# The first k-tiles of a two-layer decoder trunk in a written order, and one pair with seven products in place of two in the second group

## The chip, the cores and the metric

One program runs on one core of a Trainium2 chip. The time is the device time of one execution in microseconds (us), taken as the median of several runs. TensorE (PE) multiplies; its weight loads are shown as PEld. VectorE (DVE) and ScalarE (ACT) prepare its operands, GpSimd (POOL) raises to powers, and SyncE (SP) issues the DMAs.

## The reference, cut to what matters

A trunk of two layers on 256 tokens of 2048 values: retention, a SwiGLU feed-forward part, latent attention, and a second feed-forward part, each between two RMS norms. The change touches the first products of the retention alone:

```python
h = rms_norm(x, norm_mix_pre[0])               # x: 256 tokens x 2048
proj = h @ w_in                                # 2048 x (2048 q, 2048 k, 4096 v, 4096 g)
q, k, v, g = split(proj)
q = rope(q, positions)
k = rope(k, positions) * dk ** -0.5
scores = einsum('bhqd,bhkd->bhqk', q, k) * decay_in
```

## The kernel before

**Precision.** Every float32 matrix is split in two parts of a shorter format, hi (a cast, by ScalarE) and lo (the difference, by VectorE; `split`, L207 to L216). A product of two matrices is then three: hi by hi, hi by lo, lo by hi. A k-tile is 128 of the 2048 rows; its weight tile has 128 x 1024 values (512 KB), loaded in one DMA (`tile_load`, L543; `weights`, L218). There are two token tiles (t = 0 and 1) of 128 tokens and two halves of 512 columns (c = 0 and 1), so a k-tile takes 2 x 2 x 3 = 12 matmuls of 512 columns into four of six PSUM banks.

**The input.** x is turned by TensorE transposes in pieces of 2, 2, 4, 4 and 4 k-tiles for each token tile (`PIECES`, L577; `norm_piece`, L598). A piece is transposed into PSUM, multiplied by the norm's gains on VectorE (L608) into a tile of the "mv" slots, split into `hT`, and the squares for the norm's scale are summed one step later on ScalarE (L127). The scale itself is applied to the products afterwards.

**Groups.** The query and key part has four groups of 1024 columns (`qk_group`, L799). The first goes through `group` (L273): 16 k-tiles, all in the plain way, 192 matmuls; a `lead` of 3 lets the second token tile follow some k-tiles behind, and with `halves` = 1 the first weight tile is loaded and split in two halves of 512 columns. The other three go through `first_sevens` (L425): the first pairs of k-tiles (`QK_SEVENS` = 2 of them) are multiplied as 2 x 2 block matrices with seven products in place of eight (three matmuls each, so a pair takes 21 and not 24), the other k-tiles in the plain way. The seven need sums of blocks: of the weights for each group on VectorE (L458 to L473), of x once (`watched`, L581; `left_sums`, L244; up to three pairs are made, as the value and gate groups use three), as soon as both token tiles of a pair are there. Their results are put together in the banks by VectorE sums (L485 to L495) before the plain k-tiles are added.

**Between groups.** After each group its four banks are turned by the rotary tables on VectorE (`rotated`, L811: two multiplications a bank, L822 and L823, and four sums a token tile's two banks, L827 and L828), transposed on TensorE (L846) and multiplied to scores (L856). The tables come from `rotary_tables` (L150) after the first group: some fifteen small VectorE operations and two on ScalarE.

**Order.** The program's text gives each instruction a rank, and a planner with a cost for each instruction gives every engine's order: of what is ready by its costs, the first in the text goes first, so an operation of a later line can go ahead of one that would still wait. `later(k, fn)` (L133) puts work `k` steps on; a step passes with each weight tile that is loaded (`step`, L137). All DMAs are issued by SP in the order of the text: the identity, x of t = 0 (512 columns), the gains, two halves of weight tile 0, x of t = 1, weight tile 1, and so on. At the start 7 matmuls on zeros keep TensorE at work (`use`, L97), and 3 more come between the first transposes. Slots: 4 raw weight tiles, 5 hi and 5 lo ("whi", "wlo"), 6 "mv"; in the query and key part 3 spare tiles besides, of which a group uses one for a raw tile and two for the hi and lo of its last k-tile (`share`, L202).

## Time and profile before

| | |
|---|---|
| median of 3 runs | 2403.68 us (2402.67 to 2405.07) |
| profiled execution | 2402.24 us |
| its span | 2400.5 us |
| TensorE busy | 2383.1 us (99%) |
| VectorE busy | 2171.0 us (90%) |
| ScalarE busy | 1489.9 us (62%) |
| HBM over the span | 192 GB/s |

The span runs from the first to the last instruction; the execution's time has 1.74 us more around it. Busy time counts work and not waits; matmuls overlap, so that a matmul's own duration (about 0.39 us) is longer than the distance to the next. In the rows, `out<-in` names the tiles that an instruction writes and reads; `rqk` is the query and key part, `htp` the transposed x, `hx` that times the gains, `rx` the sums of x, `rope` the turned banks, `rtp` and `rsc` the transposes and products of the scores.

### The profile page before, as it was taken

To read this page: it belongs to the slowest core of one execution; us is meant where nothing else is said; L and a number is where in the kernel's file an instruction comes from. 1 tells how busy PE (TensorE), PEld (TensorE's weight loads), DVE (VectorE), ACT (ScalarE), POOL (GpSimd) and SP (SyncE) were. 2 spreads that over 40 slices of the span, in tenths; PEclk is the share of its full clock that TensorE was granted. 3 is DMA by queue.
4 is the path that set the end of the run, shared out by engine and by line. 5 is a ranking of instruction groups with operands and counts; after the bars stand their busy time and mean duration, and the time that the engine had idled before them with its cause. 6 is when DMAs were issued, how large, how long until landed. Compare 5 with 4: busy or idle time off the path is not lost.

```text
span 2400.5 us, 30798 instructions
## 1 busy us (share of the span) xinstructions
PE 2383.1 (99%) x10849; PEld 1969.1 (82%) x10849; DVE 2171.0 (90%) x3098; ACT 1489.9 (62%) x2104; POOL 28.6 (1%) x38
## 2 busy tenths in 40 slices
PE   9999999999999999999999999999999999999998
PEld 7888888888888888888888888887888888888887
DVE  8878989888899999999989987889999999998998
ACT  6545665665666666666666666656666665666664
POOL 0000000000001000000000000000000000000000
PEclk9999999999999999999999999999999999999999
DMA  8465465445656665656456565445666565655654
GB/s 284 166 206 192 167 209 189 165 168 190 217 187 220 210 211 188 215 180 222 153 194 215 200 197 161 128 141 168 236 200 219 177 220 184 211 166 184 220 199 168
DMA packets 129611, 463.76 MB, mean 193 GB/s; under 512 B 14640, under 2 KB 15024, under 8 KB 129456
## 3 DMA queue, kind: packets, MB, share of 16 engines
q1 hardware_dynamic: 129456, 461.80, 57.6%
q8 instruction: 85, 1.39, 0.2%
q14 instruction: 70, 0.57, 0.1%
HBM read 459.64 MB, written 2.10 MB: 192 GB/s over the span
## 4 chain that ended last, share of the span: by engine, by line
PE 92%; DVE 5%; DMA 1%; ACT 1%; issue 1%; SPq 0%; POOL 0%; DVEq 0%; POOLq 0%; ACTq 0%
PE gu_b L419 35%; PE dn_b L419 15%; PE rvg_b L419 14%; PE rto_b L419 6%; PE rqk_b L419 5%; PE dn_m L419 3%; PE q L419 3%; PE mlo_b L419 2%; PE mc_b L419 1%; PE rto_m L419 1%; PE ftp L981 1%; PE ry L909 1%; DVE xs L671 0%; PE asc L1233 0%; PE asc L1230 0%
## 5 line engine op out<-in xcount | busy, mean ns | idle before, releaser
L419 PE MATMUL gu_b<-gu_w_hi,hT 128*128 128x512 f32 x1296 | 353.5, 390 | 0.1
L419 PEld LDWEIGHTS gu_b<-gu_w_hi,hT 128*128 128x128 f32 x1296 | 242.1, 188 | 50.8 <-DVE hT L211 0.9
L210 ACT CAST dn_w_hi<-dn_w_raw 128x1024 fp32r<-128x1024 f32 (+1 forms) x176 | 169.1, 978 | 78.4 <-DMA dn_w_raw<-w_down 32.8
L419 PE MATMUL gu_b<-gu_w_lo,hT 128*128 128x512 f32 x648 | 200.2, 390 | 0.2 <-DVE gu_w_lo L211 0.2
L211 DVE TENSOR_TENSOR dn_w_lo<-dn_w_raw,dn_w_hi 128x1024 fp32r<-128x1024 f32 (+1 forms) x176 | 193.2, 1128 | 7.1 <-ACT dn_w_hi L210 6.7
L419 PE MATMUL dn_b<-dn_w_lo,dn_ah 128*128 128x512 f32 x494 | 156.7, 389 | 0.0
L419 PE MATMUL dn_b<-dn_w_hi,dn_ah 128*128 128x512 f32 x494 | 156.6, 389 | 0.0
L419 PE MATMUL rvg_b<-rvg_w_hi,hT 128*128 128x512 f32 x576 | 156.5, 390 | 0.0
L419 PE MATMUL dn_b<-dn_w_hi,dn_al 128*128 128x512 f32 x494 | 156.4, 389 | 0.0
L211 DVE TENSOR_TENSOR gu_w_lo<-gu_w_raw,gu_w_hi 128x1024 fp32r<-128x1024 f32 x122 | 143.3, 1217 | 5.3 <-ACT gu_w_hi L210 5.1
L419 PEld LDWEIGHTS gu_b<-gu_w_lo,hT 128*128 128x128 f32 x648 | 121.2, 188 | 26.6 <-DVE gu_w_lo L211 1.6
L210 ACT CAST gu_w_hi<-gu_w_raw 128x1024 fp32r<-128x1024 f32 x122 | 122.5, 1049 | 28.3 <-PE gu_b L419 11.0
L419 PEld LDWEIGHTS rvg_b<-rvg_w_hi,hT 128*128 128x128 f32 x576 | 107.8, 188 | 22.3
L210 ACT CAST gu_ahi<-gu_ta 128x1024 fp32r<-128x1024 f32 x80 | 84.4, 1055 | 46.7 <-PE gu_b L419 36.2
L211 DVE TENSOR_TENSOR gu_clo<-gu_s,gu_chi 128x1024 fp32r<-128x1024 f32 x80 | 97.4, 1219 | 14.7 <-ACT gu_chi L210 13.4
L419 PEld LDWEIGHTS dn_b<-dn_w_lo,dn_ah 128*128 128x128 f32 x494 | 92.7, 188 | 19.6 <-DVE dn_w_lo L211 0.4
L419 PEld LDWEIGHTS dn_b<-dn_w_hi,dn_al 128*128 128x128 f32 x494 | 92.7, 188 | 19.3
L419 PEld LDWEIGHTS dn_b<-dn_w_hi,dn_ah 128*128 128x128 f32 x494 | 92.7, 188 | 19.2
L419 PE MATMUL rqk_b<-rqk_w_hi,hT 128*128 128x512 f32 x384 | 106.0, 392 | 2.5 <-ACT rqk_w_hi L210 1.9
L211 DVE TENSOR_TENSOR gu_alo<-gu_ta,gu_ahi 128x1024 fp32r<-128x1024 f32 x80 | 97.7, 1221 | 6.4 <-ACT gu_ahi L210 6.4
L210 ACT CAST gu_bhi<-gu_s 128x512 fp32r<-128x512 f32 x80 | 49.7, 622 | 78.1 <-PE gu_b L419 63.2
L210 ACT CAST gu_chi<-gu_s 128x1024 fp32r<-128x1024 f32 x80 | 83.8, 1051 | 13.5 <-PE gu_b L419 13.5
(534 smaller groups left out, 6251.6 us busy)
## 6 DMA issues: line engine op xcount, KB each, us to landing
dn_w_raw<-w_down SPq DMA_DIRECT2D x176, 512.0 KB, 4.5
gu_s<-w_gu SPq DMA_DIRECT2D x160, 512.0 KB, 4.6
gu_w_raw<-w_gu SPq DMA_DIRECT2D x152, 512.0 KB, 3.7
rvg_w_raw<-ret_vg SPq DMA_DIRECT2D x67, 512.0 KB, 4.4
rto_w_raw<-ret_out SPq DMA_DIRECT2D x64, 512.0 KB, 4.3
rvg_s<-ret_vg SPq DMA_DIRECT2D x48, 512.0 KB, 4.2
rqk_w_raw<-ret_qk SPq DMA_DIRECT2D x47, 512.0 KB, 4.6
gu_w_xraw<-w_gu SPq DMA_DIRECT2D x40, 512.0 KB, 5.3
```

The costliest lines, as they stand in the source:

```text
L210: nc.scalar.copy(out=hi, in_=src)
L211: nc.vector.tensor_sub(out=lo, in0=src, in1=hi.bitcast(F32))
L419: nc.tensor.matmul(out, e[2](), e[3](), start=bank not in begun, stop=ends[bank, added.get(bank, 0)] == n, skip_group_check=bank in added,)
L909: nc.tensor.matmul(y, left, right, start=n == 0, stop=n == len(terms) - 1)
L981: nc.tensor.transpose(tp[:, b * P : (b + 1) * P], a[:, b * P : (b + 1) * P], ident)
```

## The change

The first five k-tiles of the first group, and the start, get a written order. `begin` opens a manual order for TensorE, VectorE and ScalarE. x of both token tiles is loaded in 256 columns first, between the two halves of weight tile 0, and the other 256 columns after weight tile 1; all go through SP as before. Of k-tile 0 both token tiles are multiplied by the first column half before the second half's turn. The transposes of the second pieces stand before the last three matmuls of k-tile 0, those of the third pieces behind k-tile 1. From k-tile 5 on the planner orders again; `lead` is 1. The pieces of the first eight k-tiles are kept in two spare tiles (not in "mv" slots), so this group's last k-tile has no spare room for its hi and lo. The squares of these pieces come 6 steps later, of the others 2. The sums of x come later: of the first pair 6 steps after its pieces, of the second and third 22 and 24, which is in the second group. So this group has one pair with seven products (`QK_SEVENS` = 0, 1, 2, 2), its other 14 k-tiles are plain. The rotary tables are made at k-tile 8 of the first group, the constants loaded at k-tile 6. The first group's score transposes and products come three steps later than those of the others. 6 and 2 matmuls on zeros stand in place of 7 and 3; the load of the activation table stands behind the first DMAs in the text.

```diff
 MLO_SEVENS = (3, 5), (1, 3)
-QK_SEVENS, VG_SEVENS = 2, 3
+QK_SEVENS, VG_SEVENS = (0, 1, 2, 2), 3
...
-    use(7)
+    use(6)
...
     nc.sync.dma_start(out=cst[:, C_ID : C_ID + P], in_=consts[:, C_ID : C_ID + P])
+    nc.sync.dma_start(out=xs[:, 0, 0:256], in_=xv[:, 0, 0:256])
+    nc.sync.dma_start(out=gcol, in_=gains)
+    nc.scalar.preload_act_table_set("silu_and_others")
     ident = cst[:, C_ID : C_ID + P]
...
-        def run(t, kt, cs):
-            for i, j in ((0, 0), (0, 1), (1, 0)):
+        def run(t, kt, cs, order=((0, 0), (0, 1), (1, 0))):
+            for i, j in order:
                 for c in cs:
...
         held = [[], []]
-        for kt in range(kts):
-            plan.append(("do", lambda kt=kt: load_one(kt)))
+        done, loaded = (0, 0) if begin is None else begin(plan, run, load_one, w)
+        for kt in range(done, kts):
+            if kt >= loaded:
+                plan.append(("do", lambda kt=kt: load_one(kt)))
             if kt // 2 in sevens:
...
-    def watched(pairs):
+    def watched(pairs, wait=None):
...
                     if (1 - t, p) in held:
-                        f, hi, lo = tiles[0](len(made))
-                        left_sums(*held[0, p], *held[1, p], f, hi, lo)
-                        made[p] = hi, lo
+                        if wait is None:
+                            make(p)
+                        else:
+                            later(wait(p), lambda p=p: make(p))
+        def make(p):
+            f, hi, lo = tiles[0](len(made))
+            left_sums(*held[0, p], *held[1, p], f, hi, lo)
+            made[p] = hi, lo
         watch[0] = seen
         return made, tiles
-    def norm_piece(t, i, ssq, col):
+    def norm_piece(t, i, ssq, col, room=None, wait=1):
+        norm_parts(t, i, ssq, col, room, wait)()
+    def norm_parts(t, i, ssq, col, room=None, wait=1):
         k0, n = PIECES[i]
...
         ks = slice(k0 % 4, k0 % 4 + n)
-        part = wp.tile([P, 512], F32, tag="mv", bufs=MV, name=f"hx{t}{i}")
-        part = part[:, 0 : n * P].rearrange("p (j q) -> p j q", j=n)
+        if room is None:
+            part = wp.tile([P, 512], F32, tag="mv", bufs=MV, name=f"hx{t}{i}")[:, 0 : n * P]
+        else:
+            part = room(t, k0, n)
+        part = part.rearrange("p (j q) -> p j q", j=n)
         nc.vector.tensor_tensor(
             out=part, in0=tp[:, 0 : n * P].rearrange("p (j q) -> p j q", j=n),
             in1=gcol[:, col + k0 : col + k0 + n][:, :, None].to_broadcast([P, n, P]), op=ALU.mult,
         )
-        split(hx(k0)[:, ks, 0, t, :], hx(k0)[:, ks, 1, t, :], part)
-        if watch[0] is not None:
-            watch[0](t, k0, n, part)
-        later(1, lambda: squares(xs[:, t, k0 * P : (k0 + n) * P], ssq[:, i : i + 1]))
+        def rest():
+            split(hx(k0)[:, ks, 0, t, :], hx(k0)[:, ks, 1, t, :], part)
+            if watch[0] is not None:
+                watch[0](t, k0, n, part)
+            def part_squares():
+                ins = squares(xs[:, t, k0 * P : (k0 + n) * P], ssq[:, i : i + 1])
+                if wait > 1:
+                    tc.keep_in_program_order(ins)
+            later(wait, part_squares)
+        return rest
...
+        def load_half(t, i):
+            sl = slice(i * 256, (i + 1) * 256)
+            nc.sync.dma_start(out=xs[:, t, sl], in_=xv[:, t, sl])
         def load_constants():
...
             lo = wp.tile([P, 4, P], F32R, tag="al", bufs=3, name="rxl")
             return f, hi, lo
-        ins, where = watched(max(QK_SEVENS, VG_SEVENS))
+        ins, where = watched(VG_SEVENS, lambda p: 6 + 2 * p if p < 1 else 20 + 2 * p)
         where[0] = tiles
-        load_x(0, 0)
-        later(0, lambda: norm_piece(0, 0, first[0], G_MIX))
-        later(0, lambda: norm_piece(0, 1, first[0], G_MIX))
-        later(0, lambda: use(3))
-        nc.sync.dma_start(out=gcol, in_=gains)
-        for k, c, t in ((1, 0, 1), (2, 1, 0), (3, 1, 1), (5, 2, 0), (6, 2, 1), (8, 3, 0), (9, 3, 1)):
+        pieces, spare_q = {}, [None]
+        def first_room(t, k0, n):
+            if k0 // 4 not in pieces:
+                pieces[k0 // 4] = spare_q[0](F32, f"hx{k0}")
+            a = t * 512 + k0 % 4 * P
+            return pieces[k0 // 4][:, a : a + n * P]
+        def first_parts(t, i):
+            return norm_parts(
+                t, i, first[t], G_MIX, first_room if i < 3 else None, 6 if i < 3 else 2
+            )
+        def begin(plan, run, load, w):
+            ordered = ExitStack()
+            parts = {}
+            def do(fn, *args):
+                plan.append(("do", lambda: fn(*args)))
+            def loads():
+                step()
+                ordered.enter_context(
+                    tc.manual_schedule(engines={nc.tensor.engine, nc.vector.engine, nc.scalar.engine})
+                )
+                raw = wp.tile([P, 1024], F32, tag="raw", bufs=RAW, name="rqk0_w0_raw")
+                hi = wp.tile([P, 1024], F32R, tag="whi", bufs=WB, name="rqk0_w0_hi")
+                lo = wp.tile([P, 1024], F32R, tag="wlo", bufs=WB, name="rqk0_w0_lo")
+                w[0] = hi, lo, raw
+                nc.sync.dma_start(out=raw[:, 0:512], in_=ret_qk[0, 0, :, 0:512])
+                load_half(1, 0)
+                nc.sync.dma_start(out=raw[:, 512:1024], in_=ret_qk[0, 0, :, 512:1024])
+            def half(c):
+                split(*(x[:, c * 512 : (c + 1) * 512] for x in w[0]))
+            def transposed(t, i):
+                parts[t, i] = first_parts(t, i)
+            def made(t, i):
+                parts[t, i]()
+            do(loads)
+            do(transposed, 0, 0)
+            do(use, 2)
+            do(made, 0, 0)
+            do(transposed, 1, 0)
+            do(half, 0)
+            do(made, 1, 0)
+            do(half, 1)
+            run(0, 0, (0,), ((0, 0), (1, 0)))
+            run(1, 0, (0,), ((0, 0),))
+            run(0, 0, (0,), ((0, 1),))
+            run(1, 0, (0,), ((0, 1), (1, 0)))
+            run(0, 0, (1,), ((0, 0), (1, 0), (0, 1)))
+            do(load, 1)
+            for t in range(NT):
+                do(load_half, t, 1)
+            for t in range(NT):
+                do(transposed, t, 1)
+            run(1, 0, (1,), ((0, 0), (1, 0), (0, 1)))
+            for t in range(NT):
+                do(made, t, 1)
+            do(load, 2)
+            do(load, 3)
+            for kt in range(1, 5):
+                for t in range(NT):
+                    run(t, kt, (0, 1))
+                if kt == 1:
+                    for t in range(NT):
+                        do(transposed, t, 2)
+                if kt < 3:
+                    do(load, kt + 3)
+                if kt == 1:
+                    for t in range(NT):
+                        do(made, t, 2)
+            do(ordered.close)
+            return 5, 6
+        for k, c, t in ((2, 1, 0), (3, 1, 1), (5, 2, 0), (6, 2, 1), (8, 3, 0), (9, 3, 1)):
             later(k, lambda c=c, t=t: load_x(c, t))
-        later(10, load_constants)
-        for k, t, i in (
-            (2, 1, 0), (2, 1, 1), (3, 0, 2), (3, 1, 2),
-            (7, 0, 3), (7, 1, 3), (10, 0, 4), (10, 1, 4),
-        ):
-            later(k, lambda t=t, i=i: norm_piece(t, i, first[t], G_MIX))
+        later(6, load_constants)
+        later(8, rotary_tables)
+        for k, t, i in ((6, 0, 3), (6, 1, 3), (10, 0, 4), (10, 1, 4)):
+            later(k, lambda t=t, i=i: first_parts(t, i)())
         def qk_group(gq, spare):
             name = f"rqk{gq}"
             if gq:
-                return first_sevens(h_lhs, DT, ret_qk, gq, name, QK_SEVENS, lambda p: ins[p], spare)
-            return group(h_lhs, DT, tile_load(ret_qk, gq, name, 1, spare), name, lead=3)
+                return first_sevens(h_lhs, DT, ret_qk, gq, name, QK_SEVENS[gq], lambda p: ins[p], spare)
+            return group(h_lhs, DT, tile_load(ret_qk, gq, name, 0, spare), name, lead=1, begin=begin)
         def vg_group(h, spare):
             return first_sevens(h_lhs, DT, ret_vg, h, f"rvg{h}", VG_SEVENS, lambda p: ins[p], spare)
...
+                wait = 0 if gq else 3
                 for t in range(NT):
                     for c in range(2):
-                        later(2 + t, lambda t=t, c=c: transposes(t, c))
+                        later(wait + 2 + t, lambda t=t, c=c: transposes(t, c))
                 for h2 in range(2):
-                    later(5, lambda h2=h2: products(h2))
+                    later(wait + 5, lambda h2=h2: products(h2))
             with tc.tile_pool(name="rt_q", bufs=1) as rp:
                 rope_c = rp.tile([P, NT, NF_R], F32, name="rope_c")
                 rope_s = rp.tile([P, NT, NF_R], F32, name="rope_s")
-                spare = share(3, lambda kind, name: rp.tile([P, 1024], kind, tag="spare", bufs=3, name=name))
+                spare_q[0] = lambda kind, name: rp.tile([P, 1024], kind, tag="spare", bufs=3, name=name)
+                spare = share(3, spare_q[0])
                 for gq in range(4):
-                    banks = qk_group(gq, spare)
+                    banks = qk_group(gq, spare if gq else (1, 0, spare_q[0]))
                     if gq == 0:
                         rx = [rms(first[t], D, "rx", f"first_r{t}") for t in range(NT)]
-                        rotary_tables()
                         for t in range(NT):
```

## Rows read from the trace of the kernel before

**Rows 1.** The page: the span, its first part (busy us, share of the span, instructions of each engine) and the shares of the chain that ended last by engine.

```profile
span 2400.5 us, 30798 instructions
...
PE 2383.1 (99%) x10849; PEld 1969.1 (82%) x10849; DVE 2171.0 (90%) x3098; ACT 1489.9 (62%) x2104; POOL 28.6 (1%) x38
...
PE 92%; DVE 5%; DMA 1%; ACT 1%; issue 1%; SPq 0%; POOL 0%; DVEq 0%; POOLq 0%; ACTq 0%
```

**Rows 2.** The windows of two stretches: from:to us, length, then busy us (instructions) of PE, PEld, DVE, ACT and POOL, granted clock, share of the DMA engines, GB/s.

```profile
0.00:100.00 100.00, 94.72 (x428) 74.54 (x429) 84.96 (x142) 57.36 (x86) 2.23 (x6) 1.00 0.73 254
70.00:75.00 5.00, 4.43 (x19) 3.08 (x18) 5.00 (x8) 4.91 (x6) 0.00 (x0) 1.00 0.78 274
```

**Rows 3.** TensorE's timeline of the start: start us, length us, instruction (merged where alike), in brackets the idle time before it and what ended it.

```profile
1.19 3.17 PE L99 MATMUL warm<-junk 128*128 128x512 bf16 x7 [1.19 <-DVE mhalf L115]
...
4.93 0.81 PE L99 MATMUL warm<-junk 128*128 128x512 bf16 x3
...
6.66 0.49 PE L419 MATMUL rqk_b<-rqk_w_hi,hT 128*128 128x512 f32 x1 [0.61 <-ACT hT L210]
8.58 0.50 PE L419 MATMUL rqk_b<-rqk_w_hi,hT 128*128 128x512 f32 x1 [1.43 <-ACT rqk_w_hi L210]
...
11.80 0.63 PE L602 MATMUL htp<-cst,xs 128*128 128x128 f32 x4 [0.62 <-DVE rxf L247]
12.18 1.17 PE L419 MATMUL rqk_b<-rqk_w_hi,hT 128*128 128x512 f32 x4
```

**Rows 4.** The chain that ended last in order of time, in the first group: start us, length us, what.

```profile
19.98 10.91 PE rqk_b L419 x48
30.89 0.87 PE htp L602 x8
```

**Rows 5.** TensorE's timeline: the first product of the second, third and fourth group, and of the value and gate part after them.

```profile
57.03 0.39 PE L419 MATMUL rqk_b<-rqk_bhi,hT 128*128 128x512 f32 x1
...
105.52 0.39 PE L419 MATMUL rqk_b<-rqk_bhi,hT 128*128 128x512 f32 x1
...
152.59 0.39 PE L419 MATMUL rqk_b<-rqk_bhi,hT 128*128 128x512 f32 x1
...
199.67 0.39 PE L419 MATMUL rvg_b<-rvg_bhi,hT 128*128 128x512 f32 x1
```

**Rows 6.** SyncE's timeline of the start: start us, length us of issuing, the DMA.

```profile
0.74 0.39 SPq L110 DMA_DIRECT2D cst<-consts  x1
1.18 0.42 SPq L768 DMA_DIRECT2D xs<-x  x1
...
2.12 0.91 SPq L555 DMA_DIRECT2D rqk_w_raw<-ret_qk  x2
3.07 0.43 SPq L768 DMA_DIRECT2D xs<-x  x1
3.54 0.43 SPq L555 DMA_DIRECT2D rqk_w_raw<-ret_qk  x1
```

**Rows 7.** The DMA view of the stretches in which these loads were issued, in that order: tile and source, count, KB, us from issue to landing.

```profile
cst<-consts SPq DMA_DIRECT2D x1, 64.0 KB, 1.9
...
xs<-x SPq DMA_DIRECT2D x1, 256.0 KB, 3.4
...
gcol<-gains SPq DMA_DIRECT2D x1, 52.0 KB, 3.1
...
rqk_w_raw<-ret_qk SPq DMA_DIRECT2D x1, 256.0 KB, 3.5
...
rqk_w_raw<-ret_qk SPq DMA_DIRECT2D x1, 256.0 KB, 5.3
...
xs<-x SPq DMA_DIRECT2D x1, 256.0 KB, 6.6
...
rqk_w_raw<-ret_qk SPq DMA_DIRECT2D x1, 512.0 KB, 7.4
```

**Rows 8.** The timeline of all engines: a whole weight tile's cast and subtraction.

```profile
11.01 1.05 ACT L210 CAST rqk_w_hi<-rqk_w_raw 128x1024 fp32r<-128x1024 f32 x1
...
12.54 1.22 DVE L211 TENSOR_TENSOR rqk_w_lo<-rqk_w_raw,rqk_w_hi 128x1024 fp32r<-128x1024 f32 x1
```

**Rows 9.** VectorE's groups by line and form in the first 110 us: line, operation, out<-in, shapes, count, then busy us, mean ns and idle time before them.

```profile
L462 DVE TENSOR_TENSOR rqk_ta<-rqk_s,rqk_s 128x512 f32<-128x512 f32 x4 | 2.7, 684 | 0.0
...
L179 DVE SCALAR_TENSOR_TENSOR r<-kl,r 128x320 f32<-128x320 f32 x3 | 1.5, 485 | 0.0
```

**Rows 10.** VectorE's timeline at the second group's begin (the turning's first and last operation, the subtraction of the first pair's third weight block, two of the group's own sums) and at the third group's (the turning's first operation and the first sum).

```profile
55.99 0.68 DVE L822 TENSOR_TENSOR rope_a<-rqk_b,rope_c 128x512 f32<-128x512 f32 x1
...
63.12 0.42 DVE L828 TENSOR_TENSOR rope_o<-rope_b,rope_a 128x256 f32<-128x256 f32 x1
...
65.19 1.21 DVE L211 TENSOR_TENSOR rqk_clo<-rqk_s,rqk_chi 128x1024 fp32r<-128x1024 f32 x1
66.33 0.69 DVE L488 TENSOR_TENSOR rqk_b<-rqk_b,rqk_mv 128x512 f32<-128x512 f32 x1
66.93 0.69 DVE L492 TENSOR_TENSOR rqk_b<-rqk_b,rqk_mv 128x512 f32<-128x512 f32 x1
...
105.28 0.69 DVE L822 TENSOR_TENSOR rope_a<-rqk_b,rope_c 128x512 f32<-128x512 f32 x1
...
112.75 0.68 DVE L485 TENSOR_TENSOR rqk_mv<-rqk_b,rqk_mv 128x512 f32<-128x512 f32 x1
```

More of the change, by code (lines that the diff above doesn't have):

```diff
@@ L79, in trunk @@
     nc = tc.nc
-    nc.scalar.preload_act_table_set("silu_and_others")
     sb = ctx.enter_context(tc.tile_pool(name="sb", bufs=1))
@@ L126, in squares @@
         n = src.shape[-1]
-        nc.scalar.activation(out=junk[:, 0:n], in_=src, func=AF.Square, accum_out=acc)
+        return nc.scalar.activation(out=junk[:, 0:n], in_=src, func=AF.Square, accum_out=acc)
     steps, order = [0], [0]
@@ L152, in rotary_tables @@
             posf = rp.tile([P, NT], F32, name="posf")
-            nc.vector.tensor_copy(out=posf, in_=pos_i)
+            tc.keep_in_program_order(nc.vector.tensor_copy(out=posf, in_=pos_i))
             ang = rp.tile([P, NT, NF], F32, tag="rot", bufs=7, name="ang")
@@ L273, in group @@
     def group(
-        lhs, kts, load, name, lead=2, skew=0, tail=0, banks=None, between=None, sevens=(), left=None
+        lhs, kts, load, name, lead=2, skew=0, tail=0, banks=None, between=None, sevens=(), left=None,
+        begin=None,
     ):
```

## The prediction

> **What bounds the kernel now.** I read the page first: TensorE is busy for 99% of the span, and the chain that ended last runs through it for 92% [rows 1]. So a saving counts only where TensorE waits. The windows come next: in the first 100 us TensorE is busy for 94.72 us, and within these the stretch from 70 to 75 us shows 4.43 of 5 us with VectorE busy all the time [rows 2]. The change touches nothing after the second group of the retention's query and key products, so all that it can win lies in two places: the start, and the seam between the first and the second group.
>
> The start, by TensorE's timeline [rows 3]: warming products from 1.19 us, a first real product at 6.66 us, the next at 8.58 us after waiting for a weight's cast, the last transposes at 11.80 us behind VectorE's sums, and a steady run from 12.18 us. Steady TensorE takes 10.91 us for 48 products, 0.227 us each, and 0.87 us for 8 transposes, 0.109 us each [rows 4]. The first group is 192 products and 32 transposes: 43.6 + 3.5 = 47.1 us. The second group's first product starts at 57.03 us [rows 5], so 57.03 - 47.1 = 9.9 us of the start are not work. From 12.18 us on only 44.85 - 186 x 0.2273 - 20 x 0.109 = 0.4 us of them arise; 9.5 us are the start itself.
>
> The seam, by the first product of each group [rows 5]: the second group lasts 105.52 - 57.03 = 48.49 us, the third 47.07, the fourth 47.08. The three have the same program, so 1.42 us is what the second loses to VectorE's crowding, by the rotary tables and by sums put off.
>
> **The start, step by step.** Before, the loads were issued at 0.74 to 3.54 us about 0.47 us apart [rows 6] and landed this long after their issue [rows 7]: the identity at 2.6 us, x of token tile 0 at 4.6, the two halves of weight tile 0 at 5.6 and 7.9, x of token tile 1 at 9.7, weight tile 1 at 10.9. They land in the order of issue, and by bytes: 884 KB are there at 7.9 us, 1140 KB at 9.7, 1652 KB at 10.9. The queue issues faster than the data comes, so the new order is read off the bytes. (1) The first 256 columns of tile 0 end at 192 KB, about 3.9 us; the same of tile 1 at 628 KB, 5.6 us in place of 9.7; the second half of weight tile 0 stays at 884 KB, 7.9 us; weight tile 1 ends at 1396 KB, 10.3 us; the second 256 columns of both tiles, which now stand behind it, at 1652 KB, 10.9 us. The two halves add two issues of 0.42 us to the queue; they are hidden, as the issues of x and weights lead their landings by 3 us and more.
>
> (2) TensorE's order is now written: six products of k-tile 0 on its first column half, for both tiles, then three on the second half, then the transposes of the second x pieces, then three products, then k-tile 1. The first nine need the cast and subtraction of weight tile 0's halves, some 0.6 us each after 5.6 and 7.9 us, so they are done by about 9.6 us. The transposes then hold all of TensorE until 10.9 us: this is what is late next. At 10.94 us TensorE has done 9 products and 6 transposes (the other two follow), 2.7 us of work, so it has lost 8.2 us. (3) K-tile 1 wants weight tile 1 cast (1.05 us) and subtracted (1.22 us) [rows 8], 10.3 + 2.3 = 12.6 us; TensorE is there at 10.94 + 0.22 + 5 x 0.227 = 12.3 us, so 0.3 us more is lost: 8.5 us. With the 0.4 us of the later stretch kept, 8.9 us instead of 9.9: **a gain of 1.0 us**. Bounds: if the two halves of x land at the rate of the last rows and nothing else waits, 1.8 us; if they land 1.5 us later, as one more 512 KB load would make them, a loss of 0.5 us.
>
> (4) What moves off this path: the sums of the second pair (four small ones and a split) go into the second group, the rotary tables (some fifteen operations near 0.48 us) from the seam to k-tile 8, the squares by five steps. TensorE needs 2.7 us for a k-tile there, VectorE 1.2 us for its weights, so the tables cost nothing. The pieces held for the sums take two spare tiles, so the last weight tile's two halves lose their own room; the common rooms for them number five, enough for four k-tiles of lead, and I cost it at nothing. The moved table load and two warming products fewer stand beside the wait for x.
>
> **The seam, step by step.** (5) One pair instead of two with seven products: 3 products more, +0.68 us on TensorE, with certainty. (6) VectorE loses one pair's four additions, 0.68 us each [rows 9], and one and a half extra splits of 1.22 us, and has the tables behind it; the 1.42 us can go. (7) But the pairs were also TensorE's food while VectorE turns the first group's banks. That turning starts 1.04 us ahead of the second group's first product, holds VectorE to 63.46 us (its last operation, 0.34 us after 63.12), 6.4 us after it, and goes ahead of the group's own sums [rows 10]; in the third group likewise, from 105.28 to 112.75 us. With one pair TensorE has 12 products, and 3 more on the bank whose copy ScalarE makes: 15 x 0.227 = 3.4 us. The next bank needs three sums of 0.60 us behind the turning: 6.4 + 1.8 = 8.2 us. The gap of 4.8 us can be filled by 16 transposes of the turned banks (1.75 us, the half of them ready by 2.7 us), by the one free bank's products of k-tiles 2 and 3 (1.1 us) and by a part of the score products (some 0.9 us by the rest of the group's time). I take **1.0 us** left idle; the bounds are 0 and 3.3 us (score products and k-tile 2 not ready). The change puts those transposes and scores three steps later, which matters only if an idle TensorE doesn't get them earlier; I take it that it does.
>
> (8) The second group: 47.07 + 0.68 + 1.0 = 48.75 us against 48.49: **a loss of 0.3 us** (from -0.7 to +2.6).
>
> **Sum.** -1.0 + 0.3 = -0.7 us. The profiled execution took 2402.24 us, 1.74 us over its span; it lies 1.4 us below the median of the runs, 2403.68 us. The forecast for the median is 2403.68 - 0.7, some **2403.0 us**.
>
> **The rivals.** A. *Both places come out clean*: -1.8 at the start and -0.7 at the seam, 2401.2 us. For it: VectorE gets its slack before the second group. Against it: the second pieces of x stand behind 512 KB of weights.
>
> B. *The turning starves TensorE* (slower): the 3.3 us of (7) stand, in full if the second weight half of the pair is still unsplit when the turning starts, since its subtraction then queues behind turning and sums. Seam +2.6, start -1.0: 2405.3 us. It decides from the point where the idle time between the 15th product and the first sum exceeds 1.7 us. For it: that subtraction came at 65.19 us before, after the turning. Against it: VectorE now has some 10 us less to do ahead of it.
>
> C. *The clock rises late*. The first warming products started 0.43 us apart (seven in 3.17 us), which is 1.2 GHz for 512 columns; the three at 4.93 us fit into 0.81 us, at 2.4 GHz [rows 3]. Now six run, then a gap, then two. If TensorE stayed at 1.2 GHz until the steady run, the products behind the wait for x cost 0.2 us more each; for the first dozen 2.5 us, so 2405.5 us. Against it: it was idle for most of 6.7 to 9.8 us before and kept its speed. The Trainium skill, "TensorE: Matmul & The Clock Gate", section on the HAM clock gate, says that half speed is the default and that sustained activity lifts it, which is the direction of this rival.
>
> D. *Small loads are slow*. If each of the two added loads cost the 1.9 us of the smallest one [rows 7] in turn, the second pieces would land 3.8 us later and the start would be 2.8 us worse: 2406.8 us. Against it: weight tile 1 landed 1.3 us behind the load ahead of it, with 512 KB, so loads overlap and no fixed time shows. The Trainium skill, "DMA: Bandwidth & Descriptors", section on bandwidth, asks for transfers of 1 MiB and calls those under 64 KB bound by descriptors; these rows speak for bytes, not for a price by load.
>
> E. *It does nothing that shows*, for the order written out ends at the same wait for 1652 KB: this lies within 1 us of the forecast and is counted there.
>
> **How the numbers follow.** Forecast (with E) 0.52, A 0.20, B 0.17, C 0.06, D 0.05. The range of 8 in 10 takes in A and most of B: 2401.0 to 2405.8 us. 0.2%, about what a measurement of this kernel can tell from no change, is 4.8 us; no case reaches this, for that the start's or the seam's bounds would have to meet or something unforeseen be added: faster 0.03, within 0.93, slower 0.04.
>
> **What would show it.** Of the profile after: the second group's first product near 56.0 us (step 3); the second transposes of x ended by a DMA near 10.9 us (2); the second group 48 to 49.5 us long, with idle TensorE between the 15th product and the first sum (7); later groups as long as now. I am wrong if the second x pieces land before 9.5 us, if TensorE starts the second group after 57 us, or if the third group changes by over 0.5 us.

## The result, and the profile after

| us | before | after |
|---|---|---|
| median of the runs | 2403.29 (2402.12 to 2406.29) | 2407.82 (2405.70 to 2410.66, 12 runs) |
| profiled execution | 2402.24 | 2409.92 |
| its span | 2400.5 | 2408.1 |
| second group's first product | 57.03 | 55.31 |
| length of the second, third, fourth group | 48.49, 47.07, 47.08 | 54.10, 47.06, 47.07 |

The changed kernel takes 1.0018 times as long as the one before (95% interval 1.0010 to 1.0026), 4.5 us by the medians. The forecast was 2403.0 us, with 2405.8 as the end of its range: wrong. The start gained more than forecast, 57.03 - 55.31 = 1.72 us; the second group lost 54.10 - 48.49 = 5.61 us, where 0.3 was forecast and 2.6 the bound. Together that is +3.89 us, and the value and gate part begins 203.54 - 199.67 = 3.87 us later [rows 5]. So the whole loss lies in one stretch of some 15 us. (The profiled executions lie 7.68 us apart. The other 3.8 us arise behind the start of the value and gate part, where the two programs do the same work: in the fourteen traces of this case that stretch lasts 2199.5 to 2204.6 us, 2200.8 before and 2204.6 in the change.)

**The start after.** TensorE's timeline: start us, length us, instruction, idle time before it and what ended it.

```profile
5.56 0.41 PE L617 MATMUL htp<-cst,xs 128*128 128x128 f32 x2 [0.84 <-DMA xs<-x]
5.82 0.73 PE L423 MATMUL rqk_b<-rqk_w_hi,hT 128*128 128x512 f32 x2
...
8.55 0.73 PE L423 MATMUL rqk_b<-rqk_w_hi,hT 128*128 128x512 f32 x2 [0.43 <-ACT rqk_w_hi L211]
...
10.11 0.84 PE L617 MATMUL htp<-cst,xs 128*128 128x128 f32 x4 [0.33 <-DMA xs<-x]
```

The first product starts at 5.82 us and not at 6.66, and the steady run is not held up at 11.80 us by the sums of x any more [rows 3]. The wait ahead of the second pieces' transposes ends with a DMA, as step (2) said, but near 10.1 us and not 10.9. The DMA view of the changed kernel has weight tile 1 and the two halves of x as follows; they were issued at 3.53 and 4.01 us, so they landed at 9.7 and 10.0 to 10.5.

```profile
rqk_w_raw<-ret_qk SPq DMA_DIRECT2D x1, 512.0 KB, 6.2
...
xs<-x SPq DMA_DIRECT2D x2, 128.0 KB, 6.0
```

**The seam after.** Three timelines of the same 20 us are read one behind the other. First ScalarE:

```profile
45.83 0.47 ACT L195 ACTIVATE sin_t<-rc 128x320 f32<-128x320 f32 x1 [0.53 <-DVE rc L186]
48.20 0.47 ACT L196 ACTIVATE cos_t<-rb 128x320 f32<-128x320 f32 x1 [1.90 <-DVE rb L192]
48.58 0.40 ACT L128 ACTIVATE junk<-xs 128x256 bf16<-128x256 f32 x1
...
56.61 0.62 ACT L128 ACTIVATE junk<-xs 128x512 bf16<-128x512 f32 x1
57.14 0.19 ACT L128 ACTIVATION_READ_ACCUMULATOR junk<-xs 128x1 f32 x1
57.23 0.56 ACT L485 COPY rqk_mv<-rqk_b 128x512 f32<-128x512 f32 x1
```

Eight of the ten squares of x (`junk<-xs`) stand behind the cosine of the rotary tables. Their input had landed long before, and ScalarE idles for 1.90 us ahead of the cosine, but the squares are *held*: `keep_in_program_order` ties an instruction to its place in the text on its engine, so the planner can't draw it ahead. The change has two such holds. The one on the squares stands in the diff above, in `part_squares`. The other one, on the first VectorE operation of the tables in `rotary_tables`, is part of the change too but isn't in that diff:

```diff
-            nc.vector.tensor_copy(out=posf, in_=pos_i)
+            tc.keep_in_program_order(nc.vector.tensor_copy(out=posf, in_=pos_i))
```

In the kernel before nothing held the tables, so they were not made at the seam, where the text had them: the planner had drawn their start far ahead. The line of that operation before, and the cosine there:

```profile
28.24 0.16 DVE L153 CAST posf<-pos_i 128x2 f32<-128x2 int32 x1
...
51.55 0.47 ACT L195 ACTIVATE cos_t<-rb 128x320 f32<-128x320 f32 x1
```

Then VectorE in the change:

```profile
54.43 0.68 DVE L212 TENSOR_TENSOR rqk_dlo<-rqk_t,rqk_dhi 128x512 fp32r<-128x512 f32 x1
55.80 0.16 DVE L647 TENSOR_REDUCE first_r_s<-first 128x1 f32<-128x5 f32 x1 [0.69 <-ACT junk L128]
...
56.81 0.29 DVE L991 TENSOR_SCALAR rope_c<-cos_t,first_r_r 128x128 f32<-128x128 f32 x1 [0.67 <-POOL first_r_r L123]
...
57.21 0.69 DVE L928 TENSOR_TENSOR rope_a<-rqk_b,rope_c 128x512 f32<-128x512 f32 x1
...
65.36 0.68 DVE L489 TENSOR_TENSOR rqk_mv<-rqk_b,rqk_mv 128x512 f32<-128x512 f32 x1
```

From the squares comes the norm's scale (L647), from it the scaled tables (L991), and only with these can the first group's banks be turned (L928 on). The turning starts at 57.21 us, 1.90 us *behind* the second group's first product; before, it started at 55.99, 1.04 us *ahead* of it [rows 5, 10]. The group's own first sum (L489) has to stand behind it. Last TensorE, with the first product of the second and of the third group at either end, and its windows (from:to, length, busy us of PE, PEld, DVE, ACT and POOL, granted clock, DMA share and GB/s):

```profile
55.31 0.39 PE L423 MATMUL rqk_b<-rqk_bhi,hT 128*128 128x512 f32 x1
...
56.44 0.39 PE L423 MATMUL rqk_b<-rqk_bhi,rxl 128*128 128x512 f32 x1
57.85 0.50 PE L423 MATMUL rqk_b<-rqk_chi,hT 128*128 128x512 f32 x1 [1.02 <-ACT rqk_mv L485]
...
60.79 1.52 PE L952 MATMUL rtp<-cst,rope_o 128*128 128x128 f32 x8
64.58 1.81 PE L952 MATMUL rtp<-cst,rope_o 128*128 128x128 f32 x8 [2.27 <-DVE rope_o L933]
66.19 3.23 PE L962 MATMUL rsc<-qkT 128*128 128x256 f32 x10
...
109.41 0.39 PE L423 MATMUL rqk_b<-rqk_bhi,hT 128*128 128x512 f32 x1
```

```profile
60.00:65.00 5.00, 2.72 (x16) 1.70 (x15) 5.00 (x13) 2.02 (x3) 0.00 (x0) 1.00 0.00 0
65.50:68.90 3.40, 3.40 (x13) 2.99 (x13) 3.40 (x5) 1.66 (x3) 0.00 (x0) 0.50 0.19 54
69.00:75.00 6.00, 6.00 (x28) 4.96 (x28) 4.90 (x7) 2.99 (x3) 0.00 (x0) 1.00 0.75 229
```

It waits 1.02 us for a copy that ScalarE makes behind the last square, then 2.27 us for the turned banks of the second token tile, and behind this idle time the granted clock is 0.50, the lower of its two levels, for 3.4 us: the ten score products take 3.23 us.

### The profile page after: what moved, and what is told of

Read it like the earlier page. It is cut to its first block, busy times and chain, and to the rows that moved or that the text cites. A ratio compares the mean times of both kernels' runs of the same rounds, so it can differ in the third digit from the quotient of the medians.

```text
span 2408.1 us, 30790 instructions
## 1 busy us (share of the span) xinstructions
PE 2387.9 (99%) x10850; PEld 1971.4 (82%) x10850; DVE 2168.0 (90%) x3091; ACT 1486.8 (62%) x2101; POOL 27.6 (1%) x38
## 4 chain that ended last, share of the span: by engine, by line
PE 86%; DVE 7%; DMA 3%; ACT 2%; issue 2%; SPq 0%; POOL 0%; DVEq 0%; POOLq 0%; ACTq 0%
PE gu_b L423 34%; PE rvg_b L423 14%; PE dn_b L423 13%; PE rto_b L423 5%; PE rqk_b L423 5%; PE q L423 3%; PE dn_m L423 3%; PE mlo_b L423 2%; DMA dn_w_raw<-w_down 1%; PE mc_b L423 1%; PE rto_m L423 1%; PE ftp L1089 1%; DVE gu_w_lo L212 1%; PE ry L1017 1%; DMA gu_w_raw<-w_gu 1%
## 5 line engine op out<-in xcount | busy, mean ns | idle before, releaser
L423 PE MATMUL rqk_b<-rqk_w_hi,hT 128*128 128x512 f32 x408 | 113.0, 392 | 0.8 <-ACT rqk_w_hi L211 0.4
```

The source lines that it names most:

```text
L423: nc.tensor.matmul(out, e[2](), e[3](), start=bank not in begun, stop=ends[bank, added.get(bank, 0)] == n, skip_group_check=bank in added,)
```

## The experiments

**How they are read.** Each row: the second group's first product, the first turning operation, the group's first sum (L489), the group's length and the median of the runs with the ratio to the kernel before, timed beside it. The sum is given where the kernel has the change's start and one pair. All times in us.

| kernel | first product | turning | sum | length | median | ratio, 95% |
|---|---|---|---|---|---|---|
| before | 57.03 | 55.99 | | 48.49 | | |
| the change | 55.31 | 57.21 | 65.36 | 54.10 | 2407.82 | 1.0018, 1.0010 to 1.0026 |
| 1 squares free | 55.36 | 54.98 | 62.45 | 49.76 | 2401.68 | 0.9994, 0.9985 to 1.0003 |
| 2 two pairs | 54.76 | 55.05 | | 52.51 | 2405.57 | 1.0007, 0.9998 to 1.0016 |
| 3 two pairs, squares free | 55.82 | 55.50 | | 51.85 | 2405.08 | 1.0004, 0.9995 to 1.0013 |
| 4 before, with one pair | 56.70 | 56.45 | | 49.22 | 2403.41 | 1.0002, 0.9993 to 1.0011 |
| 5 squares and tables free | 55.07 | 53.85 | 61.32 | 48.92 | 2401.41 | 0.9993, 0.9984 to 1.0002 |
| 6 as 5, two pairs | 55.27 | 54.31 | | 49.94 | 2402.87 | 1.0000, 0.9991 to 1.0009 |
| 7 as 6, tables behind the group | 54.92 | 53.53 | | 49.52 | 2401.68 | 0.9995, 0.9986 to 1.0003 |
| 8 products in the gap | 55.63 | 57.52 | 65.67 | 54.03 | 2406.88 | 1.0016, 1.0007 to 1.0025 |
| 9 tables free, squares held | 55.09 | 53.99 | 61.46 | 49.04 | 2402.00 | 0.9994, 0.9985 to 1.0003 |
| 10 as 5, scores at once | 55.10 | 53.89 | 61.36 | 48.93 | 2402.21 | 0.9993, 0.9984 to 1.0002 |
| 11 as 5, x ahead of tile 1 | 57.03 | 55.82 | 63.29 | 48.94 | 2402.51 | 0.9995, 0.9986 to 1.0004 |
| 12 transposes in the gap | 55.35 | 57.26 | 65.40 | 52.74 | 2405.88 | 1.0008, 0.9999 to 1.0017 |

*The turning* is VectorE's work on the first group's banks, and *the seam* the stretch where it overlaps the second group's first products. The theory (1): the held squares make the turning late, with one pair as the only work beside it, and the low clock follows. The first rivals: (2) one pair in place of two starves TensorE by itself; (3) the loss lies in later stages.

**1. The squares free.** In `part_squares`:

```diff
-                if wait > 1:
-                    tc.keep_in_program_order(ins)
```

> The changed kernel with one thing undone: the squares of the norm may go as early as they are ready, and are no longer pinned behind ScalarE's last traced operation. In the changed kernel they run behind the two sines of the rotary tables (48.6 to 57.2 us), the norm's scale comes at 56 us, and VectorE's turning of the first group's banks starts 1.9 us behind the second group's first product in place of 1.04 us ahead of it; the second group lasts 54.1 us. Theory 1 (late squares and one pair together, and a lower clock as a result of the idle time): the turning starts at or before the second group's first product, the clock stays up, the second group lasts 49 to 50 us, the whole 4 to 5 us less than the changed kernel, about the time of the kernel before. Theory 2 (one pair alone starves TensorE, the squares are beside the point): the second group still lasts 52 us or more, the gain under 2 us. Theory 3 (the loss lies in later stages): no change of the whole beyond 1 us.

VectorE in run 1, and TensorE's first products of the second and the third group:

```profile
54.98 0.68 DVE L926 TENSOR_TENSOR rope_a<-rqk_b,rope_c 128x512 f32<-128x512 f32 x1
...
62.45 0.68 DVE L489 TENSOR_TENSOR rqk_mv<-rqk_b,rqk_mv 128x512 f32<-128x512 f32 x1
```

```profile
55.36 0.39 PE L423 MATMUL rqk_b<-rqk_bhi,hT 128*128 128x512 f32 x1
...
105.12 0.39 PE L423 MATMUL rqk_b<-rqk_bhi,hT 128*128 128x512 f32 x1
```

The turning starts 0.38 us ahead of the first product and the group shrinks by 4.34 us to 49.76: as theory 1; theories 2 and 3 fall. (The median lies 6.1 us below the change's, more than the 4 to 5 that were expected; the two medians are of different series.)

**2. and 3. Two pairs,** with the squares held and free. Edit of 2 (3 has that of 1 as well):

```diff
-QK_SEVENS, VG_SEVENS = (0, 1, 2, 2), 3
+QK_SEVENS, VG_SEVENS = (0, 2, 2, 2), 3
-... lambda p: 6 + 2 * p if p < 1 else 20 + 2 * p)
+... lambda p: 6 + 2 * p if p < 2 else 20 + 2 * p)
```

> The changed kernel with two pairs with seven products in the second group, as before, and the sums of the second pair made in the first group; the squares stay pinned. Theory 1: the turning still starts some 2 us behind the second group's first product, but the second pair gives TensorE 12 more products to do; the second group lasts 49.5 to 51.5 us, and the clock stays up. Theory 2: with two pairs the second group lasts 48 us or less, all the loss is gone. Theory 3: no change of the whole beyond 1 us.

> Both edits together: free squares and two pairs; what is left of the change are the start, the tables made earlier, and the three steps of the scores. Theories 1 and 2: the second group lasts 47 to 47.7 us, its first product starts near 55.3 us, and the whole is 2.3 to 3.2 us less than the kernel before (2400.2 to 2401.0 us). Theory 3: the whole stays some 3 to 4 us above the kernel before.

Run 2 speaks against theory 2, which has the second pair bring the loss back. But it isn't as theory 1 either: it lies 1.0 us over that range, and its turning, expected some 2 us behind the first product, starts only 0.29 us behind it, for with the same two holds the cosine comes 3.0 us sooner than in the change.

```profile
45.18 0.47 ACT L196 ACTIVATE cos_t<-rb 128x320 f32<-128x320 f32 x1
...
55.05 0.68 DVE L928 TENSOR_TENSOR rope_a<-rqk_b,rope_c 128x512 f32<-128x512 f32 x1
```

The clock fell all the same, behind 2.26 us of idle time. So what the two holds cost depends on where the rest of the order puts the cosine, and most of run 2's loss has another cause, which run 3 shows by itself. Run 3 missed every forecast: with nothing held ahead of the turning but the tables, and two pairs, the group takes 51.85 us, again with the low clock. Its VectorE timeline shows a new wait: the second pair's weights now stand *behind* the turning.

```profile
55.50 0.68 DVE L926 TENSOR_TENSOR rope_a<-rqk_b,rope_c 128x512 f32<-128x512 f32 x1
...
62.97 0.68 DVE L463 TENSOR_TENSOR rqk_t<-rqk_ta,rqk_s 128x512 f32<-128x512 f32 x1
63.57 0.68 DVE L212 TENSOR_TENSOR rqk_blo<-rqk_s,rqk_bhi 128x512 fp32r<-128x512 f32 x1
```

A new theory: the tables, which the change holds to k-tile 8, make VectorE idle early (6.71 of 10 us busy from 20 to 30 us in run 3) and late for the second pair.

**4. One pair in the kernel before,** without anything else of the change:

```diff
-QK_SEVENS, VG_SEVENS = 2, 3
+QK_SEVENS, VG_SEVENS = (0, 1, 2, 2), 3
```

(with `QK_SEVENS[gq]` and `watched(VG_SEVENS)` where it is used)

> The kernel before with one pair with seven products in the second group and nothing else changed. Theory 1: the turning starts on time, so only the three products more (0.7 us) and a starving of 0 to 1.5 us are added, less what VectorE saves: the second group lasts 48.5 to 50 us, the whole 0 to 1.5 us more. Theory 2: the starving stands here too, 51 us or more and the whole 2.5 us or more slower.

49.22 us, 0.73 more than with two: the three products of step (5), 0.68 us, and next to nothing besides. One pair adds no starving to the 1.42 us that this seam lost already, with the turning 0.25 us ahead of the first product.

**5. to 7. The tables free.** In `rotary_tables`; 5 has besides the edit of 1, 6 those of 1 and 2, and 7 takes the tables back behind the first group:

```diff
-            tc.keep_in_program_order(nc.vector.tensor_copy(out=posf, in_=pos_i))
+            nc.vector.tensor_copy(out=posf, in_=pos_i)
```

> One pair with seven products as in the change; neither the squares nor the rotary tables are held to a place in VectorE's and ScalarE's order. Theory 1 (what is held to a late place makes the turning of the first group late): squares done by some 30 us, VectorE busy over 8.5 of 10 us between 20 and 30 us (6.8 with the tables held), turning from 53 to 55 us, second group 49.0 to 49.8 us, no low clock, median 2400.8 to 2401.8. Rival (the tables' place is of no matter, VectorE has too much to do in any order): VectorE below 7.5 of 10 us there, turning at 55 us, second group 49.8 us or more, median 2401.7 or more.

> Two pairs with seven products again, squares and rotary tables both free; the rest as in the change. Theory 1 (with the tables held to k-tile 8, VectorE idles some 3 us early and then comes late to the second pair's weights, which fall behind the turning): VectorE busy over 8.5 of 10 us between 20 and 30 us, the second pair's last subtraction ahead of the turning, second group 47.0 to 48.5 us from a first product at 55 to 56 us, no low clock, median 2399.5 to 2401. Rival (the second pair's weights are late for their load or their room, not for VectorE): that subtraction still behind the turning, second group 51 to 52.5 us with the low clock, median 2404.5 to 2405.5.

> As the run with two pairs and both free, but the rotary tables are called after the first group, as in the kernel before: of the change the start, the held pieces, the later sums and the later scores are left. Theory 1: second pair's subtraction ahead of the turning, second group 47.5 to 49 us (48.49 in the kernel before, with the same tables behind its first group), first product at 55 to 56 us, no low clock, median 2400.5 to 2402. Rival (the pairs' weights are late for load or room): 51 us or more, 2404 or more.

Run 5 came out as theory 1 forecast, its length 0.08 us below the range (VectorE 9.57 of 10 us, turning at 53.85, 48.92 us). Runs 6 and 7 came out as neither theory: VectorE is filled early (9.30 and 9.49 of 10 us), so that half of the new theory holds, but the second pair's subtractions still stand behind the turning, as the rival had it, while the groups, 49.94 and 49.52 us with the clock up, lie between the two forecasts. VectorE in run 7:

```profile
53.53 0.69 DVE L925 TENSOR_TENSOR rope_a<-rqk_b,rope_c 128x512 f32<-128x512 f32 x1
...
61.01 0.68 DVE L212 TENSOR_TENSOR rqk_blo<-rqk_s,rqk_bhi 128x512 fp32r<-128x512 f32 x1
61.61 0.68 DVE L212 TENSOR_TENSOR rqk_blo<-rqk_t,rqk_bhi 128x512 fp32r<-128x512 f32 x1
62.21 1.22 DVE L212 TENSOR_TENSOR rqk_alo<-rqk_ta,rqk_ahi 128x1024 fp32r<-128x1024 f32 x1
```

The windows of the first 55 us give a hint: VectorE is busy for 46.31 us in run 7 and for 46.19 us before, but the first group now ends 57.03 - 54.92 = 2.11 us sooner, and 1.47 of the 46.31 us are the turning itself, which begins at 53.53. What VectorE has to do ahead of the seam may thus not have got shorter with the start, so that the last of it falls behind the turning; the seam hands back 1.03 of the 2.11 us (49.52 against 48.49). No run takes VectorE's work away, so this is argued and not shown; that the weights were late for their load or their room isn't excluded.

**8. and 12. Is the low clock a cost of its own?** In 8, 20 matmuls on the tile of the warming products are put behind the third product block of the second group's first bank. (That tile holds squares by then, so in this run one bank's sums are changed.) In 12 the second bank's transposes are done over again, in `transposes` ahead of the copy:

```diff
+                    for j in range(18 if (gq, t, c) == (0, 0, 1) else 0):
+                        j %= 4
+                        nc.tensor.transpose(tp[:, j * P : (j + 1) * P], rot[2 * t + c][:, j, :], ident)
```

> The change, with 20 matmuls on zeros added after the third product group of the second group's first bank, which fall into TensorE's idle time there and add nothing to the sum. Theory (the granted clock of 0.5 for 3.4 us after the idle time is a price of its own, some 1.7 us of the 54.10): no low clock near 65 us, second group 52.0 to 52.8 us, median 2406 to 2406.5. Rival (the products of that stretch wait for VectorE at either clock, so the low clock costs nothing): second group 54 us or more even without the low clock, median 2407.8 or more.

> The change, with 18 more transposes of 128 columns behind the second bank's four (the same four, over again into the same place), which fall into the 2.27 us for which TensorE waits for the turning of the second token tile; in the earlier run the filling products took the place of transposes and so didn't settle it. Theory (the granted clock of 0.5 for 3.4 us is a price of its own): no low clock at 65 to 69 us, second transposes at 64.6 us as in the change, second group 52.4 to 53.2 us in place of 54.10, median 0.9 to 1.7 us below the change's. Rival (behind the gap TensorE waits for VectorE's sums at either clock): no low clock, but second group 53.8 to 54.3 us and the median of the change. If the clock falls all the same, it stays open.

Run 8 has no low clock and the old length, 54.03 us, as its rival forecast, but its timeline takes the verdict back: the added products ran until 65.39 us, and the first eight transposes, which stood at 60.79 us, came behind them at 65.46. So what the clock gave back can have been lost to displaced work, and the run decides nothing. Run 12 displaces nothing:

```profile
60.85 1.51 PE L952 MATMUL rtp<-cst,rope_o 128*128 128x128 f32 x8
62.19 2.13 PE L955 MATMUL rtp<-cst,rope_o 128*128 128x128 f32 x18
64.63 1.46 PE L952 MATMUL rtp<-cst,rope_o 128*128 128x128 f32 x8 [0.31 <-DVE rope_o L933]
66.09 2.01 PE L965 MATMUL rsc<-qkT 128*128 128x256 f32 x10
```

All else stands within 0.1 us of the change's trace up to 66.1 us, the granted clock stays at 1.00, the ten score products take 2.01 and not 3.23 us, and the group 52.74 us: the low clock costs 1.36 us, and 18 needless transposes win it back. (This is read from the two traces; the medians, 1.9 us apart, have intervals that overlap.)

**9. Only the tables free,** the squares held as in the change:

> The change with one line undone: the rotary tables are no longer held to k-tile 8's place, the squares still are (behind the cosine of the tables on ScalarE). Theory 1 (the price is the chain cosine, squares, sums of x, scaled tables, turning): the tables' cosine comes by 41 us as in the run with both free, the held squares behind it end by 50 us and not at 57.1, the turning starts at 53.9 to 54.7 us, second group 48.9 to 49.7 us, median 2401.3 to 2402.3. Rival (held squares cost wherever they stand, because ScalarE then comes late with casts and copies): turning at 56 us or later or the second group 51 us or more, median 2403.5 or more.

As theory 1 in all its parts. ScalarE, and below it VectorE:

```profile
40.76 0.47 ACT L196 ACTIVATE cos_t<-rb 128x320 f32<-128x320 f32 x1
...
48.87 0.19 ACT L128 ACTIVATION_READ_ACCUMULATOR junk<-xs 128x1 f32 x1
```

```profile
49.27 0.15 DVE L647 TENSOR_REDUCE first_r_s<-first 128x1 f32<-128x5 f32 x1
...
53.99 0.68 DVE L928 TENSOR_TENSOR rope_a<-rqk_b,rope_c 128x512 f32<-128x512 f32 x1
```

The squares still stand behind the cosine, but the cosine comes 7.44 us sooner, and the turning is on time. So the hold on the squares costs 0.1 us by itself (49.04 against 48.92) and that on the tables 0.8 (run 1): the rest of the price belongs to the two in a row.

**10. Scores at once** (`wait = 0` in `head_scores`, besides 5):

> As the run with one pair, squares and tables free, and besides the first group's score transposes and products no longer three steps later. If the text's place matters little, because the planner gives an idle TensorE what is ready: second group 48.6 to 49.2 us, median 2401.0 to 2401.8. Rival (the three steps hold TensorE off work that it needs while VectorE turns): second group 48.4 us or less, median 2400.9 or less.

48.93 us against 48.92 in run 5: the three steps are worth nothing either way, as the forecast took it. (The median is 0.4 us above its expectation; it was timed on another chip than run 5, together with 9 and 11.)

**11. x ahead of weight tile 1** (the two `load_half` before `load(1)` in `begin`, besides 5):

> As the run with one pair, squares and tables free, and besides the second 256 columns of x loaded ahead of weight tile 1 and not behind it. Theory (weight tile 1 with its cast and subtraction is what ends last at the start): x is there by 9.2 us, weight tile 1 0.4 to 0.8 us later than with the change's order, the second group's first product at 55.3 to 55.9 us (55.07 there). Rival, that of the prediction (the second halves of x end last): first product at 54.8 us or earlier. Median 2401.3 to 2402.2 against 2401.1 or less.

The profiled execution can't decide this. Weight tile 1 landed at 10.2 us, 0.5 later than in the change, as the theory had it. But the products came at half speed until 13.5 us and hide what that is worth; TensorE's timeline:

```profile
7.35 1.65 PE L423 MATMUL rqk_b<-rqk_w_hi,hT 128*128 128x512 f32 x3 [0.67 <-ACT rqk_w_hi L211]
8.79 1.05 PE L423 MATMUL rqk_b<-rqk_w_lo,hT 128*128 128x512 f32 x2
9.65 1.48 PE L423 MATMUL rqk_b<-rqk_w_hi,hT 128*128 128x512 f32 x3
10.93 0.63 PE L423 MATMUL rqk_b<-rqk_w_lo,hT 128*128 128x512 f32 x1
```

Nine products start from 7.35 to 10.93 us, 0.45 us apart, against 0.227 in the steady run. The medians of the same series, 2402.51 against 2402.21 in run 10, are 0.3 us apart, less than they can tell; which load ends last stays open.

## Why the prediction was wrong, point by point

**The step that failed** is (4), "the squares by five steps ... so the tables cost nothing", and through it the premise of (7), that the "turning starts 1.04 us ahead of the second group's first product". I looked for the cost of the moved work in the time that VectorE has at k-tile 8, 2.7 us against 1.2 us, and found room for the tables there; the squares, on ScalarE, I put at nothing without a reason. Of what is moved I didn't ask who waits for its result, and I passed over the two holds. I also took the tables to have stood at the seam before, in (4) and (6), where they had begun at 28.24 us; in the change they begin 1.9 us later. The squares lead through the norm's scale to the scaled tables and to the turning; held behind the cosine, which is the last of the held tables, they set when the turning begins: 1.90 us behind the first product, and the group takes 54.10 us where 48.75 were forecast.

**The loss as a sum.** A group of 47.07 us with three products more is 47.75 us (5). The rest is read off the runs, each with one cause more than the one before it:
- run 5, nothing held: 48.92, so 1.17 us are lost with one pair and the turning ahead of the group. Step (7) took 1.0 us, which comes near for the case that it assumed. That the one pair is the cause isn't shown: 0.80 us of it is one idle piece of TensorE ahead of the second token tile's transposes, and the kernel before lost 1.42 us with two pairs and 1.47 with one (run 4).
- run 1, tables held: 49.76, +0.84 us, for a turning that starts 0.38 and not 1.22 us ahead.
- run 12, tables and squares held, no low clock: 52.74, +2.98 us. The turning starts 1.91 us behind, and takes longer, because the second token tile's scale and tables fall into it (57.26 to 65.40 us, 8.14 us, against 7.47 in runs 1 and 5).
- the change: 54.10, +1.36 us, for the low clock.

That is 6.35 us over 47.75, of which the forecast had 1.0. The 5.35 us that it lacked are 0.17 + 0.84 + 2.98 + 1.36; it had no low clock in the middle of the kernel at all. One column of the table holds the sum together: in six of the runs with the change's start and one pair, the group ends 42.7 us behind its first sum (L489): 42.67 in runs 1, 5, 9 and 10, 42.68 in run 11, 42.69 in run 12. The change itself has 44.05, which is 1.36 us more, and run 8, whose added products displaced work, 43.99. So VectorE's turning sets the seam, and TensorE's products only fill it.

**The start** (1) to (3): the mechanism was right, the size off. 1.72 us and not 1.0 (1.2 to 2.3 in the ten other runs with this order of loads). The first loads landed as forecast, but weight tile 1 at 9.7 us and not at 10.3, the halves of x by 10.5 and not at 10.9: the bytes' order held, the later rate was taken some 0.5 us too slow. The DMA's wait of (2) stands ahead of the second transposes in the change and in six of these ten runs, not in the other four, so which load ends last stays open here too.

**The rivals.** B had the right place and sign and nearly the right engine: VectorE's turning starves TensorE. But its reason, an unsplit weight half, isn't there: all subtractions of the pair end by 55.1 us, ahead of the turning; and its 3.3 us came from a turning on time. (The "some 10 us less" that VectorE was to have ahead of the seam are 3.5: it is busy for 42.66 of the first 55 us, 46.19 before.) C, the late clock at the start, isn't in the change's trace, but in run 11's, where the first product of the second group came 1.96 us later than in run 5 (the other order of loads is in that figure); in run 1 the products were at half speed until 10.6 us and the second group still began at 55.36 us, 0.05 later than in the change, as far as can be told because the start waited for loads there anyway. D falls: the halves of x landed together, 6.0 us behind their issue, as the 512 KB ahead of them, 6.2. E, and A's seam, didn't come.

**What would have helped.** The forecast's own test named the right view, the second group's length; and the trace of before had the chain to follow: the last square ends at 27.1 us there, ScalarE makes the cosine at 51.6 (the line shown above), the tables are scaled by 52.5 and the turning starts at 55.99.

```profile
26.96 0.18 ACT L127 ACTIVATION_READ_ACCUMULATOR junk<-xs 128x1 f32 x1
...
52.05 0.48 DVE L883 TENSOR_SCALAR rope_c<-cos_t,first_r_r 128x128 f32<-128x128 f32 x2
```

So by that trace whatever puts the squares behind the cosine has at most the 3.5 us from the scaled tables to the turning, and VectorE is busy in these with other work.

## What to carry to other kernels

Of each step that is moved or held, ask who uses its result and when, and follow that to the engine that sets the next seam; free time on its own engine says nothing. Two holds in a row can cost far more than their sum: with one pair, each of them alone was nearly free here (0.1 and 0.8 us), together they cost 5.2 us with the clock that fell behind them. This hangs on the rest of the order: in run 2 the same two holds left the turning only 0.29 us behind the first product. And if the start gets faster, the work of the other engines ahead of the next seam has less time: runs 6 and 7 gained 1.8 to 2.1 us at the start and lost 1.0 to 1.5 in the second group, though their cause is argued only.

The change with both holds taken out (run 5) is the fastest of these kernels by its median, 2401.41 us, 2.0 us below the kernel before; its interval, 0.9984 to 1.0002, still takes in no change.

## What the runs showed of the hardware

**The clock fell in the middle of the kernel.** In the change's trace, and in those of runs 2 and 3, TensorE stood still for 2.25 to 2.27 us in one piece, and then the granted clock was 0.50 for 3.4 us. Behind 1.48 us (run 3, at the start), 1.34 us (run 1), 1.05 us (run 6) and 0.80 us (run 5) it didn't fall. In the change it cost 1.36 us on top of the 2.27. The Trainium skill, "TensorE: Matmul & The Clock Gate", part on the HAM clock gate, names for that gate two states, full speed and, for an idle engine, half speed; the stretches shown here agree, with 1.00 and 0.50.

**The clock at the start rises at another moment from one execution to the next.** TensorE was at full speed by 3.9 to 6.8 us in twelve traces, at 10.6 us in run 1 and at 13.5 us in run 11, though these two have the same warming products as the other kernels with the change's start. The same part of the skill says that this moment varies from run to run, and the traces agree. It cost next to nothing in run 1 and up to 1.96 us in run 11.
